# Rounds of two blocks and a decode row, with rows divided before they are turned, in a dilated-attention stage

## The chip, the cores and the metric

The kernel runs on one core of a Trainium2 chip. The metric is device time in microseconds of one execution, the median of several runs. The core has five engines that work side by side: TensorE (PE, with its weight loads PEld listed apart), VectorE (DVE), ScalarE (ACT), GpSimd (POOL) and SyncE (SP), which here issues most DMAs. Matrix products and transposes of PE go to PSUM, from where VectorE and ScalarE copy or process them; everything else lies in SBUF.

## The reference

The kernel is one inference step of a two-layer trunk. Layer 0 is a LongNet-style dilated attention, layer 1 a diagonal state-space layer (S5) with a GLU; each is followed by a SwiGLU feed-forward net. There are 512 prompt tokens without a cache, and 8 sample sequences of 8 tokens, each with a past of 2048 tokens whose keys and values are given. The model is 1024 wide, with 8 heads of 64 in each of three groups; everything is float32. The attention is what matters here:

```python
DIL_GROUPS = ((128, 1), (512, 4), (2048, 16))   # (window, dilation)

def dilated_block(q_blk, kv_all, qi, dilation, n_keys):
    idx = qi[:, None] - dilation * jnp.arange(n_keys)[None, :]
    valid = idx >= 0
    kvg = jnp.take(kv_all, jnp.maximum(idx, 0), axis=1)
    ...
    s = jnp.einsum('bqhd,bqkhd->bqhk', q_blk, kf) * (HEAD_DIM ** -0.5)
    s = jnp.where(valid[None, :, None, :], s, -jnp.inf)
    lse = jax.nn.logsumexp(s, axis=-1)
    p = jnp.exp(s - lse[..., None])
    return jnp.einsum('bqhk,bqkhd->bqhd', p, vf), lse
...
wts = jax.nn.softmax(jnp.stack(lses, axis=0), axis=0)
out = jnp.einsum('gbqh,gbqhd->bqhd', wts, jnp.stack(outs, axis=0))
```

Weighting the three groups by their log-sum-exp is the same as one softmax over the keys of all three groups, and the kernel computes it so: one row of exponentials per query and head, one sum, one division.

## The kernel before, in words

The stages follow each other: query, key and value projections (to about 335 us), the attention proper (`attn_phase`, 335.45 to 434.5 us), the output projection (`wo_phase`, from 435.74 us), then feed-forward, state-space layer, GLU and feed-forward. The projections of the model split each float32 operand in two halves of reduced precision and multiply three times (line 107). Inside most stages a scheduler places instructions. Inside the attention proper it does not: class `Kept` (line 661, which is why every instruction of the stage bears that line) has each instruction of VectorE, ScalarE and TensorE kept in program order. So what order these three engines work in is what order the code is written in. DMAs are issued on SP.

**Blocks.** The prompt's work is cut into 16 blocks, n = 4 hp + r, for 4 pairs of heads (hp) and 4 residues of the token index (r). A block has 128 queries and two heads; each head gives a score tile S of 128 x 512 in PSUM: 256 keys for the window with dilation 1, 128 each for the two others. A block passes through these steps:

- `scores(n)`: 8 + 4 products on PE into two S tiles.
- `masked(n)`: VectorE adds the mask and takes the row minimum, S to sm (SBUF), once per head.
- `exps(n, h)`: ScalarE's exponential in place on sm, with the row sums into den.
- `turn(n)`: PE transposes sm in four pieces per head into a tile pt of pool pP (PSUM, two buffers), so a block fills both buffers.
- `evict(n, h)`: ScalarE copies pieces 0 and 1 of pt (keys of dilation 1) to P0; pieces 2 and 3 go to P12 on VectorE for head 0 and on ScalarE for head 1. Views print both P0 and P12 as P. A copy on VectorE is made to wait for ScalarE's copy out of the same tile.
- `values(n)`: 8 products with the values of dilations 4 and 16 into O (PSUM, one buffer). At r = 3 follow 28 products for dilation 1, and the division: 16 products of ident with the reciprocals rd, broadcast, give a PSUM tile R that prints as S; ScalarE copies O to att, and VectorE multiplies att by R.

**Decode rows.** The 8 sample sequences are 8 rows. Their scores Sall exist when the stage begins. `Decode(b)` makes the softmax of row b: VectorE's maximum, ScalarE's exponential, then VectorE's reciprocal, product and a small copy (pw). It also issues the load of the row's new values, vn. `turn` transposes four pieces into a tile Sd of pool pD, from which ScalarE copies pa and pn, and VectorE spreads six strided copies into Pz. `values(part)` multiplies them with the value cache, in two parts: the cache comes in seven DMAs per row (tiles kc, one of 256 KB and six of 512 KB), whose buffers are 6 of pool kst and 4 of pool kpa, taken in turn by `turns % 10`. `out` transposes the result os once more, and VectorE copies it into att in two pieces.

**The loop.** Step n issues scores(n), the turn of block n-1, masks and exponentials of block n with the evictions of block n-1 between them, then at odd n the decode row's turn, at even n the out of the row before last, then values(n-2) and half a row's cache products. Two steps make a round: two blocks and one row. PSUM's eight banks are three for S, two for pP, one for O, two for pD.

Of the kernel before, what the change touches and what calls it, by code (L numbers as in the profile page):

```python
# [19 lines left out]
T = 512  # L20
# [643 lines left out]
def attn_phase(nc, tc, A, es, L):  # L664
# [20 lines left out]
    den, rd, S2, PT, sm, P0, P12, O = {}, {}, {}, {}, {}, {}, {}, {}  # L685

    def scores(n):
        hp, r = divmod(n, 4)
        if r == 0:
            den[hp] = wk.tile([128, 4, 2], F32, name="den")  # L690
        S2[n] = [pS.tile([128, 512], F32, name="S") for _ in range(2)]
        for b in range(4):
            for h in range(2):
                o, k = S2[n][h][b * 32:b * 32 + 32, 0:256], kT[0][half[h], hp, max(b - 1, 0) * 128:(b + 1) * 128]
                if not b:
                    o, k = o.rearrange("p (a c) -> p a c", a=2), k[:, None, :].to_broadcast([64, 2, 128])
                mm(o, qT[0][half[h], hp, r * 128 + b * 32:r * 128 + b * 32 + 32], k, start=True, stop=True, tile_position=(h * 64, b * 32))
        sl = slice(r * 128, r * 128 + 128)
        for gi in (1, 2):
            for h in range(2):  # L700
                mm(S2[n][h][:, (gi + 1) * 128:(gi + 2) * 128], qT[gi][half[h], hp, sl], kT[gi][half[h], hp, sl], start=True, stop=True)

    def masked(n):
        sm[n] = [(wk.tile([128, 512], F32, name="sm", bufs=4), wk.tile([128, 1], F32, name="nm", bufs=4)) for _ in range(2)]
        for h in range(2):
            x, nm = sm[n][h]
            v.tensor_tensor_reduce(x, S2[n][h], mp[:, n % 4, :], -SCALE, 3e38, OP.add, OP.min, nm)

    def exps(n, h):
        x, nm = sm[n][h]  # L710
        s.activation(x, x, AF.Exp, bias=nm, scale=-1.0, accum_out=den[n // 4][:, n % 4, h:h + 1])

    def turn(n):
        hp, r = divmod(n, 4)
        if r == 0:
            P0[hp] = [wk.tile([128, 2, 4, 4, 32], F32, name=f"P0_{h}", bufs=1) for h in range(2)]
        PT[n] = [pP.tile([128, 4, 128], F32, name="pt") for _ in range(2)]
        for h in range(2):
            for c in range(4):
                te.transpose(PT[n][h][:, c, :], sm[n][h][0][:, c * 128:(c + 1) * 128], ident)  # L720
        P12[n] = [wk.tile([128, 2, 128], F32, name="P12", bufs=4) for _ in range(2)]

    def evict(n, h):
        hp, r = divmod(n, 4)
        pt = PT[n][h]
        s.activation(P0[hp][h][:, :, :, r, :], pt[:, 0:2, :].rearrange("p a (b i) -> p a b i", b=4), AF.Copy)
        if h:
            s.activation(P12[n][h], pt[:, 2:4, :], AF.Copy)
        else:
            v.tensor_copy(P12[n][h], pt[:, 2:4, :])  # L730
        if h and r == 3:
            rd[hp] = wk.tile([128, 4, 2], F32, name="rd")
            v.reciprocal(rd[hp], den[hp])

    def values(n):
# [4 lines left out]
        for gi in (1, 2):  # L740
            for j in range(4):
                mm(o_[j * 32:j * 32 + 32, r], vt[gi][:, r, hp * 128 + j * 32:hp * 128 + j * 32 + 32], P12[n][j // 2][:, gi - 1, :],
                   start=gi == 1 and r == 0, stop=False, tile_position=(0, j * 32))
# [9 lines left out]
        R = pS.tile([128, 512], F32, name="S")  # L753
        for c in range(4):
# [9 lines left out]
    class Decode:  # L764
        def __init__(self, b):
# [10 lines left out]
            self.vn = dk.tile([24, 512], F32, name="vn", bufs=2)  # L776
            nc.sync.dma_start(self.vn, dram(vscr, b * 8 * 512, [[64 * 512, 3], [512, 8], [1, 512]]))

        def turn(self):
            P, Z = Sall[:, self.b], Pz[self.b % 2]  # L780
            pt = pD.tile([128, 4, 128], F32, name="Sd")
# [3 lines left out]
            self.pa = dk.tile([128, 4, 32], F32, name="pa")  # L785
            s.activation(self.pa, pt[:, 0, :].rearrange("p (a c) -> p a c", a=4), AF.Copy)
            self.pn = dk.tile([24, 128], F32, name="pn")
            s.activation(self.pn, pt[:24, 3, :], AF.Copy)
            for gi, u0, n in ((1, 0, 4), (2, 4, 8)):
                for h in range(2):  # L790
                    for m in range(8 // n):
                        j0 = h * 8 + m * n
                        base = Z[:, u0, :, j0:j0 + 1]
                        o = bass.AP(tensor=base.tensor, offset=base.offset, ap=[list(base.ap[0]), [32, 4], [129, n]])
                        v.tensor_copy(o, pt[:, gi, :].rearrange("p (a c) -> p a c", a=4)[:, :, j0:j0 + n])

        def values(self, part):
            b, Z = self.b, Pz[self.b % 2]
            if part == 0:
                self.O = pD.tile([128, 128], F32, name="Sd")  # L800
                for hp in range(4):
                    mm(self.O[hp * 32:hp * 32 + 32, :], self.pn[:, hp * 32:hp * 32 + 32], self.vn[:, hp * 128:hp * 128 + 128], start=True, stop=False, tile_position=(0, hp * 32))
            for gi, c0 in (((0, 0), (1, 0), (1, 2)), ((2, 0), (2, 2), (2, 4), (2, 6)))[part]:
                w = min(2, UNITS[gi] - c0)
                turns[0] += 1
                vc = cache_tile(nc, A, kst if turns[0] % 10 < KST else kp, "kc", gi, b, c0, w, 1)
                for c in range(w):
                    for hp in range(4):
                        pz = self.pa[:, hp, :] if self.u == 0 else Z[:, self.u - 1, hp, :]
                        mm(self.O[hp * 32:hp * 32 + 32, :], pz, vc[:, c, hp * 128:hp * 128 + 128], start=False, stop=self.u == 12, tile_position=(0, hp * 32))  # L810
                    self.u += 1
            if part == 0:
                return
            self.os = dk.tile([128, 128], F32, name="os")
            s.activation(self.os, self.O, AF.Copy)

        def out(self):
            ot = pD.tile([128, 4, 32], F32, name="Sd")
            te.transpose(ot.rearrange("p a b -> p (a b)"), self.os, ident)
# [4 lines left out]
    dec = {}  # L824
    for n in range(20):
        if n < 16:
            scores(n)
        if 1 <= n < 17:
            turn(n - 1)
# [639 lines left out]
```

## Time and profile before

| what | value |
|---|---|
| median of the runs shown | 1537.76 us (3 runs, 1534.53 to 1542.42) |
| the profiled execution, its own time | 1540.19 us |
| its span, first to last instruction | 1538.4 us |
| PE busy in the span | 97% |
| mean granted PE clock | 0.987 |
| attention proper, 335.31 to 434.50 us: PE busy | 92.89 of 99.19 us |
| the same: VectorE, ScalarE busy | 47.35, 52.68 us |
| the same: granted clock, DMA share, GB/s | 0.95, 0.83, 280 |

How to read the rows in the next sections: in a timeline, a row has the start, the length, the engine, the line, the operation with its output and inputs, shapes, and how many like it stand together; in brackets comes the idle time ahead of it and what ended it ("issue" where the profile shows nothing). In the groups by line stand the count, the busy sum in us, the mean of one in ns, and the idle time ahead. In the list of DMAs stand the queue, the count, the size of each and the median us from issue to landing. A float32 product counts as two matmuls in the trace, a transpose as one. Matmuls are pipelined, so rows of PE overlap a little: its progress is read from start to start.

### The profile page before, as it was taken

How to read it: one execution, taken by the hardware profiler on the slowest of the kernel's cores; microseconds unless marked ns; L12 is line 12 of the kernel's file. 1: busy time of each engine (PE TensorE's matmuls, PEld its weight loads, DVE VectorE, ACT ScalarE, POOL GpSimd, SP SyncE). 2: the span in 40 equal slices, each digit the busy share in tenths (PEclk: the TensorE clock that was granted, in tenths of full speed). 3: DMA queues.
4: the chain of work that ended last, by engine and by line, in shares of the span. 5: the costliest groups of instructions: out<-in, count | busy, mean ns of one | idle time of the engine just before them, and what ended most of it. 6: DMA issues, size and time to landing. Idle time of an engine off the chain costs nothing. (4 is left out here: it accounts for less than half of the span.)

```text
span 1538.4 us, 29552 instructions
## 1 busy us (share of the span) xinstructions
PE 1485.8 (97%) x12406; PEld 1391.0 (90%) x12406; DVE 902.7 (59%) x1507; ACT 521.2 (34%) x790; POOL 321.3 (21%) x368
## 2 busy tenths in 40 slices
PE   9999897898999999999999999999999999999998
PEld 7778675666799999999999999999999999999998
DVE  5899776444556954488789567853543333333342
ACT  4533444445544221222222353532332212221222
POOL 2012231220012107554344330030110001000100
PEclk9999999899999999999999999999999999999999
DMA  7599466788965655778766947965556555442222
GB/s 258 189 347 324 124 223 208 221 293 299 313 185 192 219 198 192 246 262 285 246 226 212 328 138 220 292 198 172 192 191 217 191 190 190 148 147 83 83 68 77
DMA packets 190493, 322.63 MB, mean 210 GB/s; under 512 B 39480, under 2 KB 137016, under 8 KB 188824
## 3 DMA queue, kind: packets, MB, share of 16 engines
q1 hardware_dynamic: 182888, 303.76, 58.9%
q10 hardware_dynamic: 4992, 10.04, 1.9%
q0 software_dynamic: 2480, 6.95, 1.2%
q8 instruction: 97, 1.59, 0.4%
q14 instruction: 36, 0.29, 0.1%
HBM read 289.22 MB, written 118.78 MB: 265 GB/s over the span
## 5 line engine op out<-in xcount | busy, mean ns | idle before, releaser
L101 DVE TENSOR_TENSOR wlo<-raw,whi 128x1024 fp32r<-128x1024 f32 x200 | 247.7, 1238 | 251.7 <-ACT whi L100 248.2
L100 ACT ACTIVATE whi<-raw 128x1024 fp32r<-128x1024 f32 x200 | 208.1, 1042 | 526.3 <-PE acc L107 407.6
L107 PE MATMUL acc<-xgl,whi 128*128 128x288 f32 x1760 | 379.0, 296 | 1.0 <-DVE xgl L172 1.0
L107 PE MATMUL acc<-xgh,wlo 128*128 128x288 f32 x1760 | 377.3, 295 | 0.0
L107 PE MATMUL acc<-xgh,whi 128*128 128x288 f32 x1760 | 377.1, 296 | 0.1
L107 PEld LDWEIGHTS acc<-xgl,whi 128*128 128x128 f32 x1760 | 282.6, 188 | 2.5 <-DVE xgl L172 1.3
L107 PEld LDWEIGHTS acc<-xgh,wlo 128*128 128x128 f32 x1760 | 282.9, 188 | 0.8 <-DVE wlo L101 0.4
L107 PEld LDWEIGHTS acc<-xgh,whi 128*128 128x128 f32 x1760 | 281.5, 188 | 0.7 <-DVE gt L906 0.3
L908 POOL TENSOR_TENSOR gt<-gt,rstd 128x576 f32<-128x576 f32 x44 | 77.2, 1756 | 430.4 <-ACT gt L907 430.3
L107 PE MATMUL acc<-hh,whi 128*128 128x288 f32 x704 | 151.3, 296 | 0.0
L107 PE MATMUL acc<-hh,wlo 128*128 128x288 f32 x704 | 151.1, 295 | 0.0
L107 PE MATMUL acc<-hl,whi 128*128 128x288 f32 x704 | 150.9, 295 | 0.0
L338 PE MATMUL acc<-wlo,xh 128*128 128x512 f32 x288 | 114.5, 399 | 2.8 <-DVE wlo L101 2.8
L338 PE MATMUL acc<-whi,xh 128*128 128x512 f32 x288 | 113.4, 415 | 1.3 <-ACT xh L277 1.1
L107 PEld LDWEIGHTS acc<-hh,wlo 128*128 128x128 f32 x704 | 113.0, 188 | 0.2 <-issue 0.2
L107 PEld LDWEIGHTS acc<-hl,whi 128*128 128x128 f32 x704 | 112.9, 188 | 0.2 <-issue 0.2
L107 PEld LDWEIGHTS acc<-hh,whi 128*128 128x128 f32 x704 | 113.0, 188 | 0.0
L338 PE MATMUL acc<-whi,xl 128*128 128x512 f32 x288 | 112.6, 398 | 0.0
L192 POOL TENSOR_TENSOR ssum<-ssum,sq 128x576 f32<-128x576 f32 x21 | 35.8, 1703 | 235.9 <-ACT sq L191 235.9
L338 PEld LDWEIGHTS acc<-wlo,xh 128*128 128x128 f32 x288 | 55.6, 193 | 14.5 <-DVE wlo L101 4.3
L338 PEld LDWEIGHTS acc<-whi,xh 128*128 128x128 f32 x288 | 55.2, 193 | 12.9 <-ACT xh L277 1.7
L409 DVE TENSOR_TENSOR kc<-kc 128x1024 f32<-128x1024 f32 x32 | 39.0, 1219 | 45.9 <-DMA kc<-qscr 45.9
(361 smaller groups left out, 1951.5 us busy)
## 6 DMA issues: line engine op xcount, KB each, us to landing
o_kv_s<-cache_kv_w SPq DMA_DIRECT2D x64, 1020.0 KB, 7.3
kc<-cache_kv_w SPq DMA_DIRECT2D x96, 512.0 KB, 5.8
raw<-ffn_w_gate SPq DMA_DIRECT2D x44, 512.0 KB, 4.1
raw<-ffn_w_up SPq DMA_DIRECT2D x44, 512.0 KB, 3.8
raw<-ffn_w_down SPq DMA_DIRECT2D x40, 512.0 KB, 3.5
raw<-w_qkv SPq DMA_DIRECT2D x36, 512.0 KB, 5.5
kc<-qscr SPq DMA_DIRECT2D x32, 512.0 KB, 6.1
o_kv_s<-cache_kv_w SPq DMA_DIRECT2D x16, 1008.0 KB, 6.1
```

The lines of the kernel that those rows point to most:

```text
L100: s.activation(hi, raw, AF.Copy)
L101: mark[0] = v.tensor_tensor(lo, raw, hi.bitcast(F32), OP.subtract)
L107: te.matmul(ps[:, c, :HN], w, x[:, c * HN:(c + 1) * HN], start=first and i == 0, stop=last and i == 2)
L192: g.tensor_tensor(self.ss, self.ss, sq, OP.add)
L338: ins = nc.tensor.matmul(*a, **kw)
L409: eng.tensor_tensor(kc, kc, qb, OP.mult)
L908: g.tensor_tensor(t, t, nin.r, OP.mult)
```

## The change

A round becomes the unit of the loop. Nine rounds run over i; `new` are blocks 2i and 2i+1, `old` those of the round before.

- All scores of a round come first (16 products, then 8), into four S buffers instead of three.
- The turn is by head: four transposes into one pt tile, then its copies. All four tiles of the two old blocks follow each other. P12 is copied by VectorE, except head 1 of the odd block, which ScalarE copies.
- The decode row's turn comes right behind them, and its tile is now a pt of pool pP, still of two buffers; its six Pz copies come after the next masks.
- `norms` divides a block's rows on VectorE before they are turned: a reciprocal and two products 128 x 512. R, its 16 products on PE per head pair and VectorE's product with it are gone; ScalarE's copy of O stays.
- The row's output and its transpose share one PSUM tile Od, allocated once; `out` is written ahead of the turns of the round.
- The row's cache products are one run of 52 instead of two parts, ahead of the old blocks' value products, and the seven cache tiles have 6 + 3 buffers (`turns % 9`). The load of vn moves from `Decode` to `turn`. The first decode row's softmax stands ahead of the first scores.

The diff, shortened (removed bodies stand in the listing above):

```diff
-    kp = es.enter_context(pool("kpa", bufs=4))
+    kp = es.enter_context(pool("kpa", bufs=3))
+    pS = es.enter_context(tc.tile_pool(name="pS", bufs=4, space=PSUM))
     pP = es.enter_context(tc.tile_pool(name="pP", bufs=2, space=PSUM))
     pO = es.enter_context(tc.tile_pool(name="pO", bufs=1, space=PSUM))
-    pD = es.enter_context(tc.tile_pool(name="pD", bufs=2, space=PSUM))
-    pS = es.enter_context(tc.tile_pool(name="pS", bufs=3, space=PSUM))
+    pD = es.enter_context(tc.tile_pool(name="pD", bufs=1, space=PSUM))
...
+    D = pD.tile([128, 4, 128], F32, name="Od")
...
+    def masked(n, h):
+        x, nm = sm[n, h] = wk.tile([128, 512], F32, name="sm", bufs=5), wk.tile([128, 1], F32, name="nm", bufs=6)
+        v.tensor_tensor_reduce(x, S2[n][h], mp[:, n % 4, :], -SCALE, 3e38, OP.add, OP.min, nm)
...
+    def norms(n):
+        rd = wk.tile([128, 2], F32, name="rd", bufs=4)
+        v.reciprocal(rd, den[n])
+        for h in range(2):
+            v.tensor_scalar(sm[n, h][0], sm[n, h][0], rd[:, h:h + 1], None, op0=OP.mult)
+
+    def turn(n, h):
...
+        pt = pP.tile([128, 4, 128], F32, name="pt")
+        for c in range(4):
+            te.transpose(pt[:, c, :], sm[n, h][0][:, c * 128:(c + 1) * 128], ident)
+        s.activation(P0[hp][h][:, :, :, r, :], pt[:, 0:2].rearrange("p a (b i) -> p a b i", b=4), AF.Copy)
+        P12[n, h] = wk.tile([128, 2, 128], F32, name="P12", bufs=4)
+        if n % 2 and h:
+            s.activation(P12[n, h], pt[:, 2:4], AF.Copy)
         else:
+            v.tensor_copy(P12[n, h], pt[:, 2:4])
...
-        R = pS.tile([128, 512], F32, name="S")
-        for c in range(4):
-            for j in range(4):
-                mm(R[j * 32:j * 32 + 32, c * 128:c * 128 + 128], rd[hp][:, c, j // 2:j // 2 + 1].to_broadcast([128, 32]), ident,
-                   start=True, stop=True, tile_position=(0, j * 32))
-        av = att[:, hp, :T].rearrange("p (b i r) -> p r b i", b=4, r=4)
-        s.activation(av, o_, AF.Copy)
-        v.tensor_tensor(av, av, R.rearrange("p (r b i) -> p r b i", r=4, b=4), OP.mult)
+        s.activation(att[:, hp, :T].rearrange("p (b i r) -> p r b i", b=4, r=4), o_, AF.Copy)
...
+            self.pt = pt = pP.tile([128, 4, 128], F32, name="pt")
...
+                    vc = cache_tile(nc, A, kst if turns[0] % 9 < KST else kp, "kc", gi, b, c0, w, 1)
...
+    dec = [Decode(0)]
+    for i in range(9):
+        new, old = ((2 * j, 2 * j + 1) if 0 <= j < 8 else () for j in (i, i - 1))
+        if new:
+            scores(new)
+            masked(new[0], 0)
+            if not old:
+                masked(new[0], 1)
+        if i >= 2:
+            dec[i - 2].out()
+        for n in old:
+            for h in range(2):
+                turn(n, h)
+        if new:
+            if old:
+                masked(new[0], 1)
+            dec[i].turn()
+            for h in range(2):
+                masked(new[1], h)
+            dec[i].spread()
+        for n in new:
+            exps(n)
+        for n in new:
+            norms(n)
+        if i < 7:
+            dec.append(Decode(i + 1))
+        if i:
+            dec[i - 1].values()
+        for n in old:
+            values(n)
+    dec[7].out()
```

TensorE's order in the loop step n = 4 before (S<-kT,att are the dilation-1 scores, S<-kT,qT the others, pt<-ident,sm the turn, O<-P,vt the value products, Sd<-kc the cache products):

```order
L661 MATMUL S<-kT_87,att 32x256 x8
L661 MATMUL S<-kT_88,qT_85 128x128 x2
L661 MATMUL S<-kT_89,qT_86 128x128 x2
L661 MATMUL pt<-ident,sm 128x128 x8
L661 MATMUL Sd<-ident,os 128x128
L661 MATMUL O<-P_3400,vt_2823 32x128 x2
L661 MATMUL O<-P_3401,vt_2823 32x128 x2
L661 MATMUL O<-P_3400,vt_115 32x128 x2
L661 MATMUL O<-P_3401,vt_115 32x128 x2
L661 MATMUL Sd<-vn,pn 32x128 x4
L661 MATMUL Sd<-kc,pa 32x128 x4
L661 MATMUL Sd<-kc,Pz_3193 32x128 x16
```

And the round of the change in which the first decode row's out stands:

```order
L661 MATMUL S<-kT_87,att 32x256 x16
L661 MATMUL S<-kT_88,qT_85 128x128 x2
L661 MATMUL S<-kT_89,qT_86 128x128 x2
L661 MATMUL S<-kT_88,qT_85 128x128 x2
L661 MATMUL S<-kT_89,qT_86 128x128 x2
L661 MATMUL Od<-ident,os 128x128
L661 MATMUL pt<-ident,sm 128x128 x16
L661 MATMUL pt<-ident,Sall 128x128 x3
L661 MATMUL pt<-ident,pw 24x128
L661 MATMUL Od<-vn,pn 32x128 x4
L661 MATMUL Od<-kc,pa 32x128 x4
L661 MATMUL Od<-kc,Pz_3193 32x128 x48
```

Eight transposes between scores and value products have become 16, with the four of the decode row directly behind them in the same pool, and the cache products stand in one run.

VectorE's order around a turn before, with the semaphores that each instruction waits for (Activation is ScalarE's):

```order
L661 ISA sm,nm<-S,mp 128x512 [waits PE_49]
L661 ISA nm 128x1
L661 COPY P_3845<-pt 128x256 [waits Activation_49]
L661 COPY Pz_3193<-Sd 128x4x4 [waits PE_49,Activation_49]
L661 COPY Pz_3193<-Sd 128x4x4 x3
L661 COPY Pz_3193<-Sd 128x4x8 x2
```

And in the change:

```order
L661 ISA sm,nm<-S,mp 128x512 [waits PE_49]
L661 ISA nm 128x1
L661 COPY att<-Od 64x4x8 [waits PE_49]
L661 COPY att<-Od 64x4x8
L661 COPY P_3767<-pt 128x256 [waits Activation_49]
L661 COPY P_3775<-pt 128x256 [waits Activation_49]
L661 COPY P_3783<-pt 128x256 [waits Activation_49]
L661 ISA sm,nm<-S,mp 128x512
L661 ISA nm 128x1
```

One copy of a turned tile per turn has become three in a row, each waiting for ScalarE, with one mask and the decode row's two output copies ahead of them and the other masks behind.

VectorE at the stage's end before (atl is the first work of the output projection, raw<-ldt a copy that belongs to the setup of the state-space layer, whose input comes by DMA):

```order
L661 TENSOR_TENSOR att<-att,S 128x4x128
L661 COPY att<-Sd 64x4x8 x2
L858 TENSOR_TENSOR atl<-att,ath 128x576 x4
L868 TENSOR_TENSOR xT<-acc_5033,xr 128x288
L868 TENSOR_TENSOR xT<-acc_5033,xr 128x224
L869 TENSOR_TENSOR xT<-acc_5033,xr 128x64
L1025 COPY raw<-ldt 32x128
```

And in the change:

```order
L661 COPY P_4811<-pt 128x256
L661 COPY P_4819<-pt 128x256
L661 COPY P_4827<-pt 128x256
L1029 COPY raw<-ldt 32x128
L661 COPY att<-Od 64x4x8 x2
L862 TENSOR_TENSOR atl<-att,ath 128x576 x2
```

The copy of the state-space layer's input has moved from behind the first rows of the output projection to ahead of the last decode row's output.

More of the change, by code (lines that the diff above doesn't have):

```diff
@@ L683, in mm @@
         return te.matmul(*a, skip_group_check=True, **kw)
-    den, rd, S2, PT, sm, P0, P12, O = {}, {}, {}, {}, {}, {}, {}, {}
-    def scores(n):
-        hp, r = divmod(n, 4)
[L689 to L718, printed above, removed]
-            for c in range(4):
-                te.transpose(PT[n][h][:, c, :], sm[n][h][0][:, c * 128:(c + 1) * 128], ident)
-        P12[n] = [wk.tile([128, 2, 128], F32, name="P12", bufs=4) for _ in range(2)]
@@ L723, in evict @@
[L723 to L728, printed above, removed]
-        else:
[L730 to L733, printed above, removed]
+    D = pD.tile([128, 4, 128], F32, name="Od")
@@ new lines, in attn_phase, with scores @@
+    den, S2, sm, P0, P12, O = {}, {}, {}, {}, {}, {}
+    def scores(ns):
+        for n in ns:
+            hp, r = divmod(n, 4)
+            S2[n] = [pS.tile([128, 512], F32, name="S") for _ in range(2)]
+            for b in range(4):
+                for h in range(2):
+                    o, k = S2[n][h][b * 32:b * 32 + 32, 0:256], kT[0][half[h], hp, max(b - 1, 0) * 128:(b + 1) * 128]
+                    if not b:
+                        o, k = o.rearrange("p (a c) -> p a c", a=2), k[:, None, :].to_broadcast([64, 2, 128])
+                    mm(o, qT[0][half[h], hp, r * 128 + b * 32:r * 128 + b * 32 + 32], k, start=True, stop=True, tile_position=(h * 64, b * 32))
+        for n in ns:
+            hp, r = divmod(n, 4)
+            sl = slice(r * 128, r * 128 + 128)
+            for gi in (1, 2):
+                for h in range(2):
+                    mm(S2[n][h][:, (gi + 1) * 128:(gi + 2) * 128], qT[gi][half[h], hp, sl], kT[gi][half[h], hp, sl], start=True, stop=True)
@@ new lines, in turn @@
+    def turn(n, h):
+        hp, r = divmod(n, 4)
+        if (r, h) == (0, 0):
+            P0[hp] = [wk.tile([128, 2, 4, 4, 32], F32, name=f"P0_{i}", bufs=1) for i in range(2)]
+        pt = pP.tile([128, 4, 128], F32, name="pt")
[5 more added lines that the diff above has]
+            s.activation(P12[n, h], pt[:, 2:4], AF.Copy)
+        else:
+            v.tensor_copy(P12[n, h], pt[:, 2:4])
@@ L775, in __init__, with turn @@
             v.tensor_copy(self.pw.rearrange("p (a b) -> p a b", a=3), Sall[:, b, :, 128:136])
+        def turn(self):
             self.vn = dk.tile([24, 512], F32, name="vn", bufs=2)
[L777 to L781, printed above, removed]
+            nc.sync.dma_start(self.vn, dram(vscr, self.b * 8 * 512, [[64 * 512, 3], [512, 8], [1, 512]]))
+            P = Sall[:, self.b]
+            self.pt = pt = pP.tile([128, 4, 128], F32, name="pt")
             for c in range(3):
@@ L794, in turn, with values @@
                         o = bass.AP(tensor=base.tensor, offset=base.offset, ap=[list(base.ap[0]), [32, 4], [129, n]])
-                        v.tensor_copy(o, pt[:, gi, :].rearrange("p (a c) -> p a c", a=4)[:, :, j0:j0 + n])
-        def values(self, part):
+                        v.tensor_copy(o, self.pt[:, gi, :].rearrange("p (a c) -> p a c", a=4)[:, :, j0:j0 + n])
+        def values(self):
             b, Z = self.b, Pz[self.b % 2]
[L799 to L813, printed above, removed]
@@ L814, in values @@
             self.os = dk.tile([128, 128], F32, name="os")
-            s.activation(self.os, self.O, AF.Copy)
+            s.activation(self.os, O, AF.Copy)
         def out(self):
-            ot = pD.tile([128, 4, 32], F32, name="Sd")
-            te.transpose(ot.rearrange("p a b -> p (a b)"), self.os, ident)
+            te.transpose(D[:, 2 + self.b % 2, :], self.os, ident)
+            ot = D[:, 2 + self.b % 2, :].rearrange("p (a b) -> p a b", a=4)
             q0 = T + self.b * 8
@@ L822, in out @@
                 v.tensor_copy(att[half[h], :, q0:q0 + 8], ot[half[h], :, h * 8:h * 8 + 8])
[L824 to L829, printed above, removed]
[L830 to L845 removed]
+    dec = [Decode(0)]
[9 more added lines that the diff above has]
+        for n in old:
+            for h in range(2):
+                turn(n, h)
[3 more added lines that the diff above has]
+            dec[i].turn()
+            for h in range(2):
+                masked(new[1], h)
[11 more added lines that the diff above has]
+    dec[7].out()
 def wo_phase(nc, tc, A, es, L):
```

43 lines of the change are left out of this document (23 added, 20 removed).

## The prediction

> **What bounds the kernel now.** I read the page first, for the bound of the whole, then windows around the attention stage, then the timeline of one round of it, engine by engine.
>
> ```profile
> span 1538.4 us, 29552 instructions
> PE 1485.8 (97%) x12406; PEld 1391.0 (90%) x12406; DVE 902.7 (59%) x1507; ACT 521.2 (34%) x790; POOL 321.3 (21%) x368
> ...
> 373.90:386.07 12.17, 9.92 (x217) 7.40 (x213) 5.36 (x24) 6.70 (x22) 0.00 (x0) 1.00 0.89 300
> 386.07:398.02 11.95, 11.95 (x306) 9.71 (x302) 6.39 (x24) 6.06 (x19) 0.00 (x0) 1.00 0.87 289
> 398.02:407.68 9.66, 9.66 (x218) 7.41 (x214) 5.37 (x24) 6.80 (x22) 0.00 (x0) 1.00 0.97 324
> ```
>
> The last three rows are the table by windows: the stretch, its length, busy time of PE, PEld, DVE, ACT and POOL, the granted clock, the DMA share and GB/s. Each stretch is two blocks and a decode row. PE is busy in every microsecond of two of them, VectorE and ScalarE for half of it or two thirds. So this stage is a queue of PE work. A stall that the change puts into PE's queue costs its full length, and PE work that it removes pays in full. In the first row PE misses 2.25 us, which no wait in the program explains:
>
> ```profile
> 379.93 1.69 PE L661 MATMUL Sd<-kc,Pz 128*32 128x128 f32 x50 [2.25 <-issue]
> ...
> 423.67 0.30 PE L661 MATMUL O<-P,vt 128*32 128x128 f32 x2 [0.51 <-issue]
> ```
>
> I leave these 2.76 us in place, since nothing in the change addresses them, and count ±2.8 us for them.
>
> **Term 1, PE work removed.** One round's PE order, in its timeline:
>
> ```profile
> 407.68 0.66 PE L661 MATMUL S<-kT,att 64*32 64x256 f32 x16
> 408.27 0.71 PE L661 MATMUL S<-kT,qT 64*128 64x128 f32 x8
> 408.91 1.09 PE L661 MATMUL pt<-ident,sm 128*128 128x128 f32 x8
> 409.84 0.49 PE L661 MATMUL Sd<-ident,Sall 128*128 128x128 f32 x3
> ...
> 410.37 2.17 PE L661 MATMUL O<-P,vt 128*32 128x128 f32 x72
> 412.36 1.06 PE L661 MATMUL S<-ident,rd 128*32 128x128 f32 x32
> 413.23 1.93 PE L661 MATMUL Sd<-kc,Pz 128*32 128x128 f32 x64
> ```
>
> The broadcast of the reciprocals (S<-ident,rd) holds PE from 412.36 to 413.23, 0.87 us, once per head pair: 4 x 0.87 = **-3.5 us**. All other products stay, only in another order. With them goes VectorE's product on the finished head pair, which ran beside PE.
>
> **Term 2, PE stalls added.** Blocks used to be turned one at a time: eight transposes into two pt buffers, then about 3 us or more of other PE work before the next eight. Now 16 transposes of two blocks and four of the decode row stand in a row, 20 into five tiles, and the pool still has two buffers. The third tile needs the first one's buffer, the fifth (decode) the third's. How long a buffer is held follows from these rows:
>
> ```profile
> 370.62 1.09 PE L661 MATMUL pt<-ident,sm 128*128 128x128 f32 x8
> ...
> 371.31 0.38 ACT L661 ACTIVATE P<-pt 128x256 f32<-128x256 f32 x1 [0.67 <-PE pt L661]
> ...
> 354.14 0.38 ACT L661 ACTIVATE P<-pt 128x256 f32<-128x256 f32 x1 [5.19 <-PE pt L661]
> ...
> 354.55 0.42 DVE L661 COPY P<-pt 128x256 f32<-128x256 f32 x1 [0.15 <-ACT P L661]
> ...
> 341.24 0.43 DVE L661 TENSOR_SCALAR Sall<-Sall,drd 128x408 f32<-128x408 f32 x1
> ...
> 341.72 0.55 PE L661 MATMUL Sd<-ident,Sall 128*128 128x128 f32 x3 [0.42 <-DVE Sall L661]
> ```
>
> Four transposes begin at 370.62 and ScalarE takes the tile up at 371.31: 0.69 us. Its copy takes 0.38. VectorE's copy of the other half comes behind it (354.14 + 0.38 = 354.52, start 354.55): 0.03 + 0.42. PE takes up 0.05 after VectorE (341.67 to 341.72). Together 1.57 us until the buffer can be written again. In that time PE has eight transposes, which in the round above take from 408.91 to 409.84, 0.93 us. The stall is 0.64, say 0.65 us. The fourth tile comes 0.47 us after the third and finds its buffer ready at that moment. So two stalls in each of the rounds 2 to 7 and one in the last, which has no decode row to turn: 13 x 0.65 = **+8.5 us**. Round 1 belongs to the head, below. Behind the waiting transpose stand the decode row, its cache products, the value products and the next scores, and ScalarE's and VectorE's copies wait for them in turn. VectorE's copy is the last to come because the program makes it wait for ScalarE's. If it did not, the stall would be 0.65 - 0.41 = 0.24, and 13 of them 3.1 us: the lower bound. The upper bound is a stall lengthened by VectorE's two copies of the decode row standing in front (0.39 us, below): 13 x 1.0 = 13 us.
>
> The Trainium skill speaks to that order too. In "PSUM — Partial Sum Buffer", section "PSUM bank collisions raise a hardware error", it says that ScalarE and VectorE may not read one bank and quadrant at the same time. By it the lower bound cannot happen; the 0.03 us between the two copies above agrees.
>
> **Term 3, what moves under cover.** The division of the rows is 32 new products on VectorE. The nearest rows:
>
> ```profile
> L661 DVE TENSOR_SCALAR Sall<-Sall,drd 128x408 f32<-128x408 f32 x5 | 2.2, 432 | 0.2
> ...
> L661 DVE CUSTOM_DVE_ANT_0 sm<-S,mp 128x512 f32<-128x512 f32 x20 | 13.0, 686 | 4.2 <-PE S L661 4.0
> ```
>
> 432 ns x 512/408 = 0.54 us each, so 2.2 us per round and two small reciprocals. They follow the exponentials and come before the next round's transposes. From the third copy on VectorE has the rest of that copy (0.3), three masks of 0.65 (13.0 / 20), the decode spread (0.6), the division (2.6), the next decode row with its wait for ScalarE (2.0), a mask and the out copies (1.0): about 8.5 us up to the next round's first copy. PE comes round to it in about 9 us in a short round and 10.5 in a long one. So cost 0, with some 0.5 us of cover in short rounds. If it is gone, it is PE's first copy that comes late (rival 3). The exponentials, now four in a row, have no earlier user.
>
> The V cache loads now leave SP in one burst per round and have nine buffers instead of ten.
>
> ```profile
> kc<-cache_kv_w SPq DMA_DIRECT2D x43, 512.0 KB, 6.3
> ...
> kc<-cache_kv_w SPq DMA_DIRECT2D x7, 256.0 KB, 4.5
> ```
>
> A decode row is six tiles of 512 KB and one of 256 KB, 3.4 MB. At 324 GB/s with a share of 0.97, hence 334 at full share, that is 10.2 us, and a short round will take 9.66 + 1.3 = 11.0. The burst frees the buffers some 9 us before they are read again, against 6.3 us to landing. Cost 0, but little cover.
>
> **Term 4, the head.**
>
> ```profile
> 335.31 0.74 DVE L378 SCALAR_TENSOR_TENSOR a<-acc,rr,ks 64x512 f32<-64x512 f32 x1
> ...
> 336.79 0.69 DVE L661 CUSTOM_DVE_ANT_0 sm<-S,mp 128x512 f32<-128x512 f32 x1 [0.74 <-PE S L661]
> ...
> 337.57 1.28 ACT L661 ACT_TABLE_LOAD   x1 [2.94 <-DVE nm L661]
> ...
> 347.93 0.65 PE L661 MATMUL Sd<-vn,pn 24*32 24x128 f32 x8 [2.07 <-DMA vn<-vscr]
> ...
> 357.44 0.66 PE L661 MATMUL S<-kT,att 64*32 64x256 f32 x16
> ```
>
> The score buffers now lie on banks whose last reader ends at 336.05, so PE starts 0.6 us later than at 335.45. Decode row 0 now goes first on VectorE. Its exponential waits for the 1.28 us table load, so the first mask comes near 339.3 instead of 336.79. Then masks, exponentials, norms and row 1 stand between the first scores and the third tile. I lay that chain out to 348.0, where PE stalls about 3.2 us, in place of the 2.07 us for vn. PE's remaining work of round 1 ends between 354.5 (full clock) and 357.2 (half clock as before, where the stage ran at 0.50 until 354.41). At 357.44 the old order had turned one block more, 0.93 us. So -2.0 to +0.7; I take 0, as the new idle time, too, will cost clock.
>
> **Term 5, the tail.**
>
> ```profile
> 431.77 1.93 PE L661 MATMUL Sd<-kc,Pz 128*32 128x128 f32 x64
> 434.16 0.33 PE L661 MATMUL Sd<-ident,os 128*128 128x128 f32 x1 [0.46 <-ACT os L661]
> ...
> 434.53 0.39 DVE L661 COPY att<-Sd 64x32 f32<-64x32 f32 x2 [1.05 <-PE Sd L661]
> ...
> 433.76 0.41 SPq L1021 DMA_DIRECT2D raw<-ssm_a_re  x1
> ...
> dcol<-ssm_d SPq DMA_DIRECT2D x1, 4.0 KB, 3.5
> ...
> raw<-ssm_a_re SPq DMA_DIRECT2D x1, 16.0 KB, 1.7
> ```
>
> Today PE's last products end at 433.70 and the output projection starts at 435.74, 2.04 us later. In the change VectorE's copy of ssm_log_dt stands ahead of the last decode copies, and its load is the third on SP behind the end of the last P12 products. Call that end X. PE goes on with 56 products and the transpose until X + 1.8. The load is issued at X + 0.3 + 2 x 0.47 and lands 1.7 to 3.5 us later; then 0.2, 0.39 and ScalarE's first 0.7. The projection starts at X + 4.3 to X + 6.1, which is 2.5 to 4.3 us after PE's last work. So +0.5 to +2.3; I take **+1.3**.
>
> **Sum.** -3.5 + 8.5 + 0 + 0 + 1.3 = **+6.3 us**. The profiled execution took 1540.19 us (span 1538.4 and 1.8 around it), so 1546.5 in its terms. It lay 2.4 us above the median of the runs shown, so 1544 as a median. The lower ends give -3.5 + 3.1 - 2.0 + 0.5 - 2.8 = -4.7, the upper ones -3.5 + 13 + 0.7 + 2.3 + 2.8 = +15.3.
>
> **Rivals.** (1) *No stall worth its name; not slower.* If the two buffers come free before PE is back, the 8.5 us go and -3.5 + 1.3 = -2.2 remain: **1535.5**. It decides from a stall of 0.17 us down (13 x 0.17 = 3.5 - 1.3). For it: in the old order PE hardly ever waits for pt. Against: there PE always had other work between two blocks.
>
> (2) *The clock halves in the rounds.*
>
> ```profile
> 374.88:378.30 3.42, 2.80 (x48) 1.00 0.97 331
> 378.30:381.71 3.41, 1.78 (x58) 1.00 0.68 211
> 381.71:385.12 3.41, 3.41 (x69) 1.00 0.94 321
> 432.91:436.33 3.42, 1.71 (x37) 1.00 0.49 83
> 436.33:439.74 3.41, 3.41 (x16) 0.50 0.85 341
> ```
>
> These rows show PE alone. After a stretch with 1.71 of 3.42 us busy the next ran at 0.50; after 1.78 it did not. In the change a stretch over the 20 transposes has about 2.1 of 3.41 us busy, above both. If it counts for less, each of seven rounds has a stretch at half clock, which costs up to 1.7 us, and with some of it lost in stalls anyway about 10 us: **1554**. The Trainium skill ("TensorE: Matmul & The Clock Gate", section "Part 4: PE-mode transpose") says that transposes do not count as PE-busy in the same way; by it this would happen every round. Against it, the stretch at 374.88 held 1.46 us of transposes and kept the clock.
>
> (3) *VectorE or the V loads become the bound in the short rounds.* Each has cover of about 0.5 to 0.8 us there. Missing it by 1 us in the three or four short rounds gives **1548**.
>
> **How the numbers follow.** Forecast 0.56, rival 1 0.12, rival 2 0.14, rival 3 0.18. The forecast's own range, with term 2 between 0.5 and 0.8 us a stall and the ends of the head and tail, is 1539 to 1550. For 8 in 10 I go to 1535 and 1554, which takes in most of rivals 1 and 2. A measurement of this kernel tells about 0.5% from no change, here 7.7 us, thus 1530.1 and 1545.5. Above 1545.5 lie a third of the forecast (0.19), nearly all of rival 2 (0.13) and most of rival 3 (0.14): 0.46. Below 1530.1 lies only a part of rival 1 with the 2.76 us gone: 0.06. The rest, 0.48.
>
> **What would show it.** In the new profile, PE's pt<-ident,sm and pt<-ident,Sall should show idle time ended by VectorE's P copy, near 0.65 us, about 13 times; rounds of about 11.0 and 12.4 us against 9.7 and 11.95; no S<-ident,rd; granted clock 1.00 from round 2 on; the first projection product 2.5 us or more after the last transpose. I am wrong if pt shows no waits (rival 1), if the clock drops inside the rounds (rival 2), if PE's waits end on kc or on sm's division (rival 3), or if the head loses more than a microsecond.

## The result, and the profile after

The change makes the kernel slower: 1541.48 us, median of 20 runs (1538.35 to 1544.03), against 1535.87 for 20 runs of the kernel before beside it. The ratio is 1.0034, 95% interval 1.0023 to 1.0044, so 3.5 to 6.8 us more. Forecast were +6.3.

The profiled execution took 1543.31 us (span 1541.5), 3.1 more than that of before. That difference can't be read as it stands. The program ahead of the attention stage is the same in all kernels of this text, yet its last product begins anywhere from 328.8 to 334.6 us in their profiles. So traces are compared from that product on (the last Sd<-kT,Q, at 334.24 before, 334.01 after) to the matmul that stands 100 behind the first of the output projection, counted in the trace. That **stretch** is 116.24 us before and 119.11 after. The profile prints 2.76 us of "issue" for before (the two rows in the prediction) and 0.28 for after. But the idle time in brackets leaves out part of what a gap costs. The gap of after, in PE's timeline:

```profile
411.21 0.65 PE L661 MATMUL S<-kT,att 64*32 64x256 f32 x12
412.15 1.05 PE L661 MATMUL S<-kT,att 64*32 64x256 f32 x20 [0.28 <-issue]
413.13 1.16 PE L661 MATMUL S<-kT,qT 64*128 64x128 f32 x16
```

These 32 take 1.92 us from start to start, 1.03 in the other rounds: the gap costs 0.9. Taken so, against the same products elsewhere in the profile, the two gaps of before cost 2.6 and 0.9. Without the **gaps** the stretch is 112.7 against 118.2: +5.5, about what the runs measure.

PE's waits in the attention stage of the changed kernel, grouped by what ended them (total us, times, longest):

```profile
PE pt L661 <- DVE P L661: 7.7, 15, 0.6
PE acc L107 <- ACT ath L861: 3.6, 1, 3.6
PE pt L661 <- DVE Sall L661: 2.2, 1, 2.2
...
PE Od L661 <- DMA kc<-cache_kv_w: 1.3, 2, 0.7
...
PE S L661 <- issue: 0.3, 1, 0.3
```

The kernel before has no wait of PE for P. Now there are 15, 13 of them from round 2 on as forecast and two in round 1. PE's timeline of a short round (one without the dilation-1 products of a head pair), from its scores to the next:

```profile
389.24 1.09 PE L661 MATMUL S<-kT,att 64*32 64x256 f32 x32
390.27 1.16 PE L661 MATMUL S<-kT,qT 64*128 64x128 f32 x16
391.36 0.33 PE L661 MATMUL Od<-ident,os 128*128 128x128 f32 x1
391.52 1.04 PE L661 MATMUL pt<-ident,sm 128*128 128x128 f32 x8
393.12 1.09 PE L661 MATMUL pt<-ident,sm 128*128 128x128 f32 x8 [0.56 <-DVE P L661]
394.71 0.55 PE L661 MATMUL pt<-ident,Sall 128*128 128x128 f32 x3 [0.50 <-DVE P L661]
395.09 0.27 PE L661 MATMUL pt<-ident,pw 128*24 128x128 f32 x1
395.30 0.42 PE L661 MATMUL Od<-vn,pn 24*32 24x128 f32 x8
...
395.89 2.80 PE L661 MATMUL Od<-kc,Pz 128*32 128x128 f32 x96
398.51 1.06 PE L661 MATMUL O<-P,vt 128*32 128x128 f32 x32
399.50 1.09 PE L661 MATMUL S<-kT,att 64*32 64x256 f32 x32
```

From start to start the first eight transposes take 1.60 us and the next eight 1.59, where 0.93 were needed: two stalls of 0.66. Over the 13 places the loss is 8.4 us (intervals of 1.53 to 1.60, minus 0.93). But the scores of two blocks take 391.36 - 389.24 = 2.12 us. Before, one block took 408.91 - 407.68 = 1.23, two 2.46. The cache products, from the vn row to the value products, take 3.21 instead of 3.44. Of before, in its timeline (the first part starts at 413.23, in the prediction):

```profile
415.09 0.66 PE L661 MATMUL S<-kT,att 64*32 64x256 f32 x16
...
418.26 0.42 PE L661 MATMUL Sd<-vn,pn 24*32 24x128 f32 x8
...
419.84 0.66 PE L661 MATMUL S<-kT,att 64*32 64x256 f32 x16
```

That is 1.86 + 1.58. The work is the same; it stands in longer runs. So a short round takes 10.26 us (389.24 to 399.50) and the next, a long one, 11.71, where 11.0 and 12.4 were forecast.

The end of the stage in the same timeline:

```profile
425.68 2.13 PE L661 MATMUL Od<-kc,Pz 128*32 128x128 f32 x64
428.46 0.65 PE L661 MATMUL Od<-kc,Pz 128*32 128x128 f32 x16 [0.66 <-DMA kc<-cache_kv_w]
429.74 0.65 PE L661 MATMUL Od<-kc,Pz 128*32 128x128 f32 x16 [0.64 <-DMA kc<-cache_kv_w]
430.20 2.58 PE L661 MATMUL O<-P,vt 128*32 128x128 f32 x88
432.72 0.33 PE L661 MATMUL Od<-ident,os 128*128 128x128 f32 x1
436.64 1.81 PE L107 MATMUL acc<-ath,whi 128*128 128x288 f32 x6 [3.59 <-ACT ath L861]
...
449.32 0.50 PE L107 MATMUL acc<-ath,whi 128*128 128x288 f32 x2 [1.35 <-DVE xT L873]
```

And VectorE's timeline there:

```profile
435.30 0.22 DVE L1029 COPY raw<-ldt 32x128 f32<-32x128 f32 x1 [9.70 <-DMA ldt<-ssm_log_dt]
435.44 0.38 DVE L661 COPY att<-Od 64x32 f32<-64x32 f32 x2
...
446.70 1.23 DVE L101 TENSOR_TENSOR wlo<-raw,whi 128x1024 fp32r<-128x1024 f32 x1 [7.19 <-ACT whi L100]
447.96 1.08 DVE L872 TENSOR_TENSOR xT<-acc,xr 128x288 f32<-128x288 f32 x2
```

VectorE stands still until 435.30 for ssm_log_dt, with the last decode row behind it. The first projection product comes 3.92 us after the last transpose (before: 435.74 - 434.16 = 1.58). And there is a second displacement that I had not looked for: a weight split (wlo) now stands ahead of VectorE's first sums, and PE waits 1.35 us for the sums.

The account, without the gaps, in us against before: up to the first scores of round 2, -1.1 (with 0.93 allowed for the block that before has already turned there); from there to the last transpose +2.6; then +2.3 to the projection and +1.7 within it, of which the wait for the sums is about 1.5 from start to start. Sum +5.5.

### The profile page after: what moved, and what is told of

It reads as the page before. It is cut to its first block, busy times and chain, and to the rows that moved or that the text cites. A ratio compares the mean times of both kernels' runs of the same rounds, so it can differ in the third digit from the quotient of the medians.

```text
span 1541.5 us, 29284 instructions
## 1 busy us (share of the span) xinstructions
PE 1477.9 (96%) x12278; PEld 1387.2 (90%) x12278; DVE 916.8 (59%) x1555; ACT 522.2 (34%) x782; POOL 321.4 (21%) x368
## 3 DMA queue, kind: packets, MB, share of 16 engines
q8 instruction: 96, 1.57, 0.4%
```

## The experiments

Each was timed beside the kernel before. "Stretch" is the one above. "Issue" is what the profile prints, "gaps" what it costs from start to start, "rest" the stretch without the gaps. There is one profile for each kernel. The diffs are shortened and commented; what else moves with the lines shown stands in the expectations.

| run | ratio to before, 95% interval | stretch, us | issue | gaps | rest |
|---|---|---|---|---|---|
| the kernel before | 1 | 116.24 | 2.76 | 3.5 | 112.7 |
| the change | 1.0034 (1.0023, 1.0044) | 119.11 | 0.28 | 0.9 | 118.2 |
| e1_products_first | 1.0003 (0.9987, 1.0020) | 116.61 | 0.76 | 1.4 | 115.2 |
| e2_both_stalls | 1.0014 (1.0001, 1.0028) | 117.61 | 5.02 | 7.0 | 110.6 |
| e3_ldt_pool | 1.0007 (0.9993, 1.0021) | 116.58 | 1.72 | 2.3 | 114.2 |
| e4_division_alone | 1.0011 (0.9991, 1.0031) | 117.62 | 1.10 | 1.9 | 115.7 |
| e5_one_v_tile | 0.9982 (0.9968, 0.9996) | 111.11 | 0 | 0 | 111.1 |
| e6_scores_by_block | 1.0048 (1.0033, 1.0063) | 120.97 | 0.60 | 1.2 | 119.8 |
| e7_fill_and_tail | 1.0013 (0.9995, 1.0031) | 114.72 | 1.32 | 1.9 | 112.8 |
| e8_all | 1.0006 (0.9991, 1.0022) | 117.02 | 4.49 | 6.0 | 111.0 |
| e9_before_one_v_tile | 1.0004 (0.9982, 1.0026) | 115.58 | 0 | 0 | 115.6 |
| e10_after_one_v_tile | 1.0018 (1.0001, 1.0035) | 115.15 | 0 | 0 | 115.2 |
| e11_division_reordered | 0.9991 (0.9970, 1.0012) | 114.11 | 6.00 | 8.8 | 105.3 |

One thing in "rest" does not follow from the order alone. The granted clock stood at 0.50 for 3.4 us in the projection or at its start in most runs, before and the change among them, for 6.8 us in e1, and not there in e3, e4 and e11. In before a pair of projection products takes 0.48 us in that stretch and 0.26 behind it, so the stretch costs about 1.6 us.

**The stalls.** e1 fills the second stall of a round:

```diff
-            dec[i].turn()            # behind turn(old)
...
+        if i:
+            dec[i - 1].values()      # products first
+        if new:
+            dec[i].turn()
```

> The change, with the cache products of the old decode row moved ahead of the turn of the new row, so that 3.2 us of PE work stand between the fourth pt tile and the fifth (the masks, exponentials and divisions are written ahead of the row's copies, so that nothing new waits for them). Theory A (each wait for a pt buffer costs PE its full length): the second of the two stalls of a round goes, 0.63 us in six rounds, 3.8 us: 1.0011 of the kernel before against 1.0034 for the change, about 1537.6 us, with no idle time ahead of pt<-ident,Sall and still some 0.5 us ahead of the third pt<-ident,sm. Theory B (the rounds are bound by VectorE or by the V loads, and the stall only shows where PE waits for them): the time stays at 1541.5, and a like wait turns up elsewhere on PE.

Measured is 1.0003, and PE's waits for P in the stage fall from 15 to 8, as the grouped waits of e1 show:

```profile
PE pt L661 <- DVE P L661: 5.2, 8, 1.6
```

None is left ahead of pt<-ident,Sall. The rest is 3.0 us shorter than the change's; from the first scores of round 2 to the last transpose it is 3.7, where 3.8 were forecast. Theory A holds.

e2 fills both:

```diff
+        for h in range(2) if old else ():
+            turn(old[0], h)
...
+            dec[i - 1].values(0)
+            turn(old[1], h)          # both h
...
+            dec[i - 1].values(1)
+            dec[i - 2].out()
+            dec[i].turn()
```

> As the last one, and the products cut in two: one part stands between the turns of the two old blocks, the other ahead of the row's turn, so that no three pt tiles follow each other; the row's transposed output comes behind them. Theory A: both stalls go, 13 x 0.63 = 8.2 us less than the change, minus about 0.1 us per round for the cut, 0.7 us: 1534 us, 0.9988 of before; rounds of about 11.0 and 9.3 us, no idle time ahead of any pt. Theory B (VectorE's 8.5 us of work per round or the V loads bound it): 1538 or more, with PE waiting for sm or kc.

No pt waits for P any more (one waits 1.41 us for a copy of Pz instead), and the rest is 110.6, 7.6 us below the change's, 6.1 of it from round 2 to the last transpose. But the time is 1.0014, not 0.9988. From the grouped waits of e2 on PE:

```profile
PE O L661 <- issue: 3.0, 2, 2.0
...
PE S L661 <- issue: 1.2, 1, 1.2
PE Od L661 <- issue: 0.9, 2, 0.6
```

Five gaps have come in, printed as 5.0 us and costing 7.0, in which PE waits for nothing that the program names. The trace's DMA records show what precedes their ends. The instructions of the engines arrive in 16 KB packets on a queue of their own, and in each case the last of these landed 1.36 to 1.54 us before PE went on (gaps ending at 355.95, 362.42, 368.75, 386.65 and 409.43; landings at 354.55, 360.90, 367.39, 385.11 and 408.04). The two gaps of before fit too (379.93 and 423.67; 378.31 and 422.22). Such a packet lands about every 6 us, so this is no accident. Theory A was right about the stalls and blind to what takes their place. Theory B's wait for sm or kc did not turn up.

**Why the instructions come late.** e5 is e2 with one value tile per row:

```diff
-                vc = cache_tile(nc, A, ..., "kc", gi, b, c0, w, 1)
+                if gi == 0:
+                    self.vc = cache_tile(nc, A, ..., "kc", 1, b, 0, 2, 1)
+                vc = self.vc
```

> The kernel without the two stalls (products cut in two), but each decode row loads a single tile of its value cache, 0.5 MB instead of 3.4, and uses it for all its products: most of the value cache is left out of the computation, the instructions of TensorE, VectorE and ScalarE stay. In the full version PE stood five times on "issue", 5.0 us in all, and each time it went on 1.3 to 1.6 us after a 16 KB packet of its instructions had landed. Theory C (the instruction packets come late since they share the DMA engines with the value tiles): the issue gaps go, and the stage from the first scores to the first projection product takes about 94.2 us instead of 99.2; the whole 0.998 of before. Theory D (PE, no longer stalled, runs through its instructions faster than they are fetched, whatever else the DMA engines do): gaps of 4 to 5 us stay, and the ratio stays near 1.0014.

All gaps are gone, and the ratio is 0.9982. First scores to first projection product is 92.75 us, less than the 94.2 forecast: the stretch is 6.5 us shorter than that of e2, near the 7.0 that the gaps cost there from start to start. That rules for C: in this stage PE's instructions come late only where value tiles are loaded beside them. In the ten profiles with full loads there is always at least one gap in the stage (0.28 to 6.00 us printed), in the three with one tile none. Whether the packets queue behind the tiles or are asked for late is not shown.

**The order of the products.** e6 ungroups the scores:

```diff
         for n in ns:
...
-        for n in ns:
-            hp, r = divmod(n, 4)
             sl = slice(r * 128, r * 128 + 128)
```

> The change, with the score products written block by block as before (8 of dilation 1, 4 others, 8, 4) instead of 16 and 8. In the change the scores of two blocks take PE 2.12 us, before 2 x 1.23 = 2.46 us, though the products are the same. If PE loses some 0.1 us at each switch between kinds of product, 2.46 comes back, 0.34 us in each of eight rounds, 2.7 us in all: ratio 1.0052 against the change's 1.0034. If the difference comes from somewhere else (what runs beside it), 2.12 stays and so does the time.

PE's timeline of e6, the second block's scores of a round:

```profile
399.41 0.66 PE L661 MATMUL S<-kT,att 64*32 64x256 f32 x16
...
400.65 0.33 PE L661 MATMUL Od<-ident,os 128*128 128x128 f32 x1
```

One block's scores are back at 1.24 us (400.65 - 399.41), as before. The time moves the same way, 1.0048, though against the change this is within the intervals; the rows decide. The round has two switches between kinds of product less in the change, and 0.36 us (2.48 - 2.12) less work for it, so about 0.18 us a switch. For the cache products e2 gives the same test: cut in two, they take 1.58 and 1.90 us (377.33 to 378.91, 379.94 to 381.84), 3.48 instead of 3.21.

**The tail.** e3 takes the waiting copy off VectorE:

```diff
-            v.tensor_copy(raw[:, 2]..., ldt...)
+            g.tensor_copy(raw[:, 2]..., ldt...)
```

> The change, with the copy of ssm_log_dt on GpSimd instead of VectorE, so that VectorE's queue no longer waits for that load ahead of the last decode row's output. If the tail's cost is that wait, the first projection product comes about 1.6 us after the last transpose instead of 3.92, and the whole is 2.3 us shorter: 1539.2, ratio 1.0019. PE's wait of 1.35 us for xT in the projection, behind a weight split that VectorE now has ahead of it, should stay. If instead ScalarE's copy of O is what the projection waits for, nothing moves: 1541.5.

PE's timeline of e3, from the last transpose:

```profile
432.41 0.33 PE L661 MATMUL Od<-ident,os 128*128 128x128 f32 x1
434.15 1.06 PE L107 MATMUL acc<-ath,whi 128*128 128x288 f32 x6 [1.41 <-ACT ath L861]
...
445.59 0.50 PE L107 MATMUL acc<-ath,whi 128*128 128x288 f32 x2 [1.60 <-DVE xT L873]
```

The distance falls from 3.92 to 1.74 us, the forecast 2.2; the wait for xT stays. VectorE's wait for the load was the cost of the tail. The ratio, 1.0007, is lower than the forecast 1.0019, which lies within its interval. The rest is 4.0 us below the change's; the clock of the projection, which did not fall to 0.50, explains most of what is beyond the 2.2.

e7 adds this to e1 and takes the split of w_o's weights off VectorE:

```diff
+        wh, wl = load_w(A["w_o"], D, 0, 4, c * 256, 256, 0.0, g)   # wlo on GpSimd
```

> The kernel with the cache products ahead of the decode row's turn, and both things that delayed the output projection undone: the copy of ssm_log_dt on GpSimd, and the low halves of w_o's weights subtracted on GpSimd, so that VectorE has no weight split ahead of its sums for xT. From 1.0003: minus 2.2 us for the first and 1.35 us for the second if both are paid in full by PE, 0.998, about 1535.9 where before is 1538.9. If PE only meets its next late instruction packet instead, 1.000.

The timelines of e7, of SP's queue, of VectorE and of PE:

```profile
426.82 0.72 SPq L863 DMA_DIRECT2D xr<-x_scr  x1
```

```profile
436.88 1.08 DVE L878 TENSOR_TENSOR xT<-acc,xr 128x288 f32<-128x288 f32 x2 [6.28 <-DMA xr<-x_scr]
```

```profile
438.24 0.82 PE L107 MATMUL acc<-ath,whi 128*128 128x288 f32 x2 [2.28 <-DVE xT L879]
```

The first repair holds, the second bought nothing: with the split gone, VectorE's sums wait for xr, 2304 KB, whose load is issued at 426.82 behind the loads of the state-space setup and lands 10 us later. PE waits 2.28 us instead of 1.35. So one late thing had hidden another. Timed, e7 can't be told from e1 or from before.

e8 joins e2, both repairs and ten value buffers (`bufs=4`, `% 10`; sm with four):

> The kernel without either stall, with both repairs of the tail as in the last one, and with ten value buffers again (four sm buffers instead of five make the room). From 1.0014 minus 3.5 us: 0.9991. If late instruction packets take what the stalls give (5.0 us in the profile without the repairs), it is no faster than the version that fills only one of the two stalls, and its profile shows at least 3 us of issue in the stage.

1.0006, with 4.49 us of issue, 3.60 in one gap of PE's timeline of e8:

```profile
386.14 1.34 PE L661 MATMUL O<-P,vt 128*32 128x128 f32 x18 [3.60 <-issue]
```

Not to be told from e1, as its second case says. What the stalls give, late instructions take: the rest is 7.2 us below the change's, the gaps cost 5.1 more. And right behind the long gap the granted clock stood at 0.50 for one stretch of 3.4 us (386.26 to 389.67).

**The division.** e4 is the kernel before with the division alone:

```diff
+        if n < 16:
+            norms(n)                 # behind exps(n, 0), exps(n, 1)
...
-        R = pS.tile([128, 512], F32, name="S")   # and its products
-        v.tensor_tensor(av, av, R..., OP.mult)
```

> The kernel before with one thing of the change: rows divided on VectorE right behind their exponentials, no broadcast of reciprocals on PE, no product of att with it. If the division lies under cover in any order, the 3.5 us of PE work come out in full: 1532.4, ratio 0.9977. If it needs the advance by a round, PE's transposes (of the block, or of the decode row whose softmax stands behind the division on VectorE) wait for VectorE some 1 to 2 us per round: 1541 to 1549, ratio 1.003 to 1.008, with idle time of PE ended by DVE sm or DVE Sall.

PE's grouped waits in the stage of e4:

```profile
PE Sd L661 <- DVE Sall L661: 5.9, 6, 1.2
PE pt L661 <- DVE sm L661: 3.3, 5, 1.5
```

The ratio, 1.0011, lies between the two cases. The trace speaks for the second: the 3.5 us are out, and so are the 2.1 that PE waited for vn; waits of 5.9 and 3.3 us for VectorE are in, and the rest is 3.0 us longer than before's (115.7 against 112.7). In that order the division is not under cover. In e11 it is put elsewhere:

```diff
-            dec[n // 2] = Decode(n // 2)          # at even n, whole
+            dec[n // 2 + 1] = Decode(n // 2 + 1)  # at odd n, to the exponential
...
+            dec[n // 2].divide()                  # at even n, behind masked(n)
...
+            evict(n - 1, 0); exps(n, 0); exps(n, 1); evict(n - 1, 1)
+            norms(n, 0); norms(n, 1)
```

> The kernel before with the division on VectorE and no broadcast, as in the run of the division alone, whose PE waited 0.85 to 1.24 us a round for the decode row's softmax and 0.31 for the block's rows. Here the decode row's exponential starts half a round earlier and its division stands behind the next masks; each head's rows are divided by themselves; and ScalarE does both exponentials of a block ahead of the second eviction. If the price of the division alone was its place in VectorE's and ScalarE's order, these waits go and the 3.5 us of the broadcast come out: 0.9977, about 1532.4 of 1536, with no S<-ident,rd on PE. If two blocks' advance is needed for the division to lie under cover, it stays near 1.001, with PE waiting for sm or Sall.

PE's grouped waits of e11:

```profile
PE Sd L661 <- issue: 5.7, 6, 1.3
PE pt L661 <- DVE rd L661: 1.7, 1, 1.7
```

The waits for Sall are gone, and one wait for a division is left, in the first round. The rest is 105.3 us, 7.4 below before's. From the first scores of block 4 to the last transpose it is 3.3 shorter, the broadcast's 3.5 or nearly so. Ahead of them it is 3.7 shorter: the 2.1 us for vn don't show there either, 1.7 are waited for the division, and the clock stood at 0.50 for 6.8 us instead of 10.2. The other 0.4 lie in the projection. So the division doesn't need the advance. But seven late packets cost 8.8 us (6.0 printed), more than in any other run, and the time is 0.9991 (0.9970 to 1.0012): faster than the change, not to be told from before.

**Without the value loads.** e9 and e10 are before and the change with e5's diff.

> The kernel before, but each decode row loads one tile of its value cache (0.5 MB) and uses it for all its products; most of the value cache is left out. Reference for the next run. PE's issue gaps of the stage (2.76 us in the profile of before) should be gone, if value tiles delay the instruction packets: about 2 us off, 0.9985.

> The change, with the same left out. If the change's cost is what stands on PE's own queue (R -3.5, two pt stalls a round +8.2, fewer switches between kinds of product -3.7, head -1.4, tail +2.3, projection waiting for its sums +1.4), it stays 3.3 us slower than the last run. If it came from the value tiles (their burst, nine buffers instead of ten, the instruction packets behind them), both take the same time.

Neither has an issue gap. By time, 1.0004 and 1.0018, the difference of 2 us is smaller than the intervals, so this pair does not decide by time, and e9 does not show the 2 us that it was expected to save (0.9985 lies within its interval). By trace the two stretches are alike (115.58, 115.15), not 3.3 apart. One reason lies in e9: a copy of the state-space setup (here cwd<-cw) stands ahead of the last decode row's copies there too, and the weight split ahead of the sums, as VectorE's timeline of e9 shows.

```profile
426.51 0.23 DVE L1088 COPY cwd<-cw 128x128 f32<-128x128 f32 x1 [1.76 <-DMA cw<-ssm_c_re]
426.65 0.38 DVE L661 COPY att<-Sd 64x32 f32<-64x32 f32 x2
...
437.87 1.22 DVE L101 TENSOR_TENSOR wlo<-raw,whi 128x1024 fp32r<-128x1024 f32 x1 [7.27 <-ACT whi L100]
439.45 1.08 DVE L870 TENSOR_TENSOR xT<-acc,xr 128x288 f32<-128x288 f32 x2 [0.36 <-DMA xr<-x_scr]
```

Its projection starts 2.66 us after the last transpose (before: 1.58), and from there the 100 matmuls take 16.76 us instead of 14.74. So e9 was no clean reference for the tail. Up to the last transpose it is one: it takes 96.16 us, and before, without the gaps, 96.4. There the change with one tile is 0.6 us ahead (95.51), while with full loads it is 1.4 behind (97.8 against 96.4). From round 2 on it is 0.5 us slower with one tile and 2.6 with full loads. In between lie the two waits for kc, which cost 1.9 us from start to start (425.68 to 430.20 is 4.52 us; the same products take 2.62 in the round shown above).

## Why the prediction was right

**Term 1, the broadcast.** Right: no S<-ident,rd in the profile after, 3.5 us out.

**Term 2, the stalls.** Right in place, number and size: 13, 0.60 to 0.67 us, 8.4 in sum against 8.5, ended by VectorE's copy. e1 and e2 show that filling the gaps removes them. That the rate lies in the chain of the two copies was only argued: no run shortened the copies.

**"All other products stay, only in another order."** The step that failed. The order had a price: in longer runs the same products take 0.34 us less for the scores of a round (shown by e6) and 0.23 less for the cache products (e2). The balance from round 2 to the last transpose, +2.6 = -3.5 + 8.4 + 1.9 (V waits) - 0.5 (before's wait for os) - rest, leaves about 3.7 us for it; six rounds of scores and seven of cache products make 3.7 as well. Between e9 and e10, without V waits, the same balance leaves 3.9. I had carried the duration of a run of 16 or 64 matmuls over to runs twice as long. That is the larger part of the 0.7 us by which the rounds came out shorter than forecast.

**Term 3, cover.** The division cost nothing: PE never waits for sm from round 2 on. The V loads had less cover than I gave them, in the last round only, the one that has no scores ahead; kc cost 1.9 us there. That the missing scores are the reason is not tested.

**Term 4, the head.** -1.1 where I took 0, within my -2.0 to +0.7. The stall of 3.2 us laid out at 348.0 is not there (0.6 us at 348.78); PE waited 2.2 us for Sall at 340.29. And the new idle time did not cost clock in sum: 0.50 for 6.8 us of the head, in before for 10.2.

**Term 5, the tail.** The mechanism is right (e3), the size 2.3 us, the upper end of +0.5 to +2.3, since ssm_log_dt was taken up 2.58 us after the last transpose. That a weight split would also move ahead of the sums, 1.7 us within the projection, I had not read from the order, where it stood.

So the sum, +6.3 against +5.5 in the traces and about 5.2 timed, is right partly by luck, because things that I missed cancel: 3.7 us less in the rounds, 3.6 more from kc and the projection.

**Rivals.** The first falls: the buffers are not free in time. The second falls: stretches full of transposes kept the clock. Of after, PE's windows (stretch, length, PE busy and count, clock, DMA share, GB/s):

```profile
392.21:395.62 3.41, 2.36 (x24) 1.00 1.00 372
395.62:399.03 3.41, 3.41 (x128) 1.00 0.49 161
402.45:405.86 3.41, 2.42 (x28) 1.00 1.02 379
```

Of the first row's 2.36 us 2.10 are transposes, and the next stretch ran at 1.00. The rule of the Trainium skill ("TensorE: Matmul & The Clock Gate", "Part 4: PE-mode transpose"), by which they do not count as busy in the same way, is not borne out here for float32 transposes: 0.26 of 3.41 us would have been left. The third rival was true for the last round alone.

## What to carry to other kernels

Before a pool of two buffers is fed by work that has been put in one run, write down how long a buffer is held and how long the producer takes for the others: here 1.57 against 0.93 us gave each stall to within 0.04. Fill such a gap with other work of the same engine, and then look at what the engine meets next: in e2 late instructions took back 6.1 of 7.6 us. Read the cost of a gap from start to start: for 22 of the 23 late-packet gaps the idle time that the profile prints was 0.2 to 0.6 us less than the delay of the products around it. Read the new order past the edited function as well: 4 of the 5.5 us arose in code that the diff does not touch.

## What the runs showed of the hardware

- PE's instructions come in 16 KB packets through the DMA engines while the kernel runs. In all ten profiles with full value loads at least one packet was late in the attention stage; PE went on 1.2 to 1.6 us after it had landed, in all 23 gaps. In the three with about a sixth of the loads none was. By and large, the faster PE's order was without them, the more they cost, from start to start: 0.9 us in the change, 7.0 in e2, 8.8 in e11.
- Two switches of PE fewer between kinds of float32 score products saved 0.36 us in a round, and one run of cache products instead of two 0.23 to 0.27.
- The stage ahead, whose program is the same in all, ends between 328.8 and 334.6 us. One profile against another can't show 5 us in the whole; a stretch between two fixed instructions can.
